# Expert gates of a product-key mixture: one 256-column matmul a token for both parts of the gate

## The chip, the cores and the metric

One core of a Trainium2 chip runs the whole program in one launch. The metric is device time in microseconds (us), a median over runs. A profiled execution of the same program gives the rows shown below.

## What is computed

The reference is a stack of layers on 256 tokens of width 1024 (retention, differential attention, feed-forward blocks, a recurrent mixer), all in float32. Two of its layers hold a product-key expert block, and only that block is touched here:

```python
q = (xc @ w_q).reshape(PEER_CHUNK, PEER_HEADS, 2, half)
sc = jnp.einsum('thpd,hpnd->thpn', q, subkeys)
s1, i1 = lax.top_k(sc[:, :, 0], PEER_TOPK)
s2, i2 = lax.top_k(sc[:, :, 1], PEER_TOPK)
cand = s1[..., :, None] + s2[..., None, :]          # best 16 of 256 per head
...
gate = jax.nn.softmax(top, axis=-1)
act = jax.nn.gelu(jnp.einsum('ted,td->te', u_e, xc))
return jnp.einsum('te,ted->td', gate * act, v_e)
```

There are 8 heads with 16 experts each, so every token has 128 slots; the experts form a 128 x 128 grid (i1, i2).

## The kernel before

The kernel computes the activations of all 16,384 experts densely and multiplies them by a gate that is zero for experts not chosen. `H` is an SBUF tile of 128 partitions (i1) x 128 rows (i2) x 256 tokens in float32. The method `peer` runs once for each of the two layers, in these stages:

- **Query stage.** 16 weight units through `gemm_a`, key scores and the first top-k (`route_keys`).
- **Expert stage, called the u stage here.** A loop over `i2` from 0 to 127. Each unit is one 128 x 1024 weight block, loaded by a DMA into one of four `raw` buffers and split by `split` into a high part `wh` (ScalarE, L122) and a low part `wl` (VectorE, L123) in three buffers each. `gemm_a` (L144 to L146) then does 24 matmuls of 256 columns into a `mm` accumulator (two banks). A gelu on ScalarE (L1234, L1236) empties it into `H`, or, for tokens whose gate is there already, into the buffer `ge`, which VectorE multiplies onto `H` (L1237).
- **Routing**, spread over units 2 to 43 (`route`): it ends with `rt["T"]`, four float16 values for each slot and token: i1, i2, and the gate's high and low part.
- **Gates**, from unit 44 on: 64 groups of four tokens per layer. `onehots` builds, for four tokens at once, the one-hot of i1 (`o1`), the one-hot of i2 (`o2`) and its products with the two gate parts (`oh`, `ol`), all 128 slots x 128 x 4 tokens in float16 with the token innermost. `gates` then does, for each token, two matmuls of 128 columns that add up in one accumulator: `o1` is the stationary operand, `oh` and `ol` are the moving ones. Because the token is innermost, both operands are read at a step of four float16 values, 8 bytes. The four tokens share one `aux` bank. One unit later `apply(k)` reads that bank twice: VectorE multiplies it onto the `k` rows of `H` that exist (L1441), ScalarE copies the remaining rows (L1444), to be multiplied when their unit's gelu comes.
- **Value stage.** 128 units of `peer_v`, with `H` as stationary operand (L1260) and four `acc` banks.

Each engine runs its instructions in the order of its own queue. That order comes from a planner that simulates the program; the splits have priority over what surrounds them (`AHEAD`). All weight DMAs go through SyncE's queue (SP), in order. Routing uses the part of `H` from row `K0` = 44 on as scratch memory (`carve`), since those rows are not filled yet; `consts_peer` loads three constant tables at the start of the block.

Of the kernel before, what the change touches and what calls it, by code (L numbers as in the profile page):

```python
# [67 lines left out]
class Ker:  # L68
# [27 lines left out]
    def psum(s, ctx, mm, aux, acc):  # L96

        for n, c in (("mm", mm), ("aux", aux), ("acc", acc)):
            setattr(s, "p" + n, ctx.enter_context(
                s.tc.tile_pool(name=f"ps_{n}", bufs=c, space=PSUM, reuse_waits="tile")))  # L100
        s.naux = aux
        s.cyc = ([s.aux, s.mm, s.aux] if aux > 2 else [s.aux, s.mm])
        s.psn = 0
# [1058 lines left out]
    def peer(s, l, xs, units_q, units_u, units_v, ln):  # L1162
        nc, A = s.nc, s.A
        with ExitStack() as cx:
            s.psum(cx, 2, 2, 4)
            hp = s.pool("peer_h", 1, cx)
            H = hp.tile([128, NKEYS, T], F32, name="H")
            cu = ExitStack()
            po = s.pool("peer_oh", 2, cu)
            p = s.pool("peer_u", 1, cu)  # L1170
            p2 = s.pool("peer_u2", 2, cu)
            s.consts_peer(p)
            xT = s.x_transposed(p, xs, "xT", s.ln_cols(ln), p2)

            off = [K0 * T]

            def carve(shape, dt=F32):
# [7 lines left out]
                if len(shape) == 2:  # L1185
# [2 lines left out]
                return ap.rearrange("p (%s) -> p %s" % (" ".join(names), " ".join(names)),  # L1188
                                    **{k: v for k, v in zip(names, shape[1:])})

            def restart():
                off[0] = K0 * T

            carve.restart = restart
            qT = carve([128, 16, T])
# [14 lines left out]
            for c in range(16):  # L1210
                ps = bank(c)
                s.gemm_a(next(units_q), xT, ps)
                nc.scalar.activation(qT[:, c], ps, AF.Copy)
                if c == 2:
                    scores(0)
                if c > 1:
                    scores(c - 1)
                    s.route_keys(rt, sc, c - 2)
            route = s.route(carve, p, rt)
            g = 0  # L1220
            pend = []
            for i2 in range(NKEYS):
# [7 lines left out]
                if nt == 0:  # L1230
                    nc.scalar.activation(H[:, i2], ps, AF.Gelu_apprx_tanh)
                else:
                    if nt < T:
                        nc.scalar.activation(H[:, i2, nt:], ps[:, nt:], AF.Gelu_apprx_tanh)  # L1234
                    ge = p2.tile([128, T], F32, name="ge")
                    nc.scalar.activation(ge[:, :nt], ps[:, :nt], AF.Gelu_apprx_tanh)  # L1236
                    nc.vector.tensor_tensor(H[:, i2, :nt], H[:, i2, :nt], ge[:, :nt], op=ALU.mult)  # L1237
                if 2 <= i2 < K0:
# [5 lines left out]
                elif i2 >= K0:  # L1244
                    for f in pend:
                        f(i2 + 1)
                        g += 1
                    e = (i2 + 2 - K0) * (T // 4) // (NKEYS - KEND - K0)
                    pend = [s.gates(H, s.onehots(p, po, rt, j * 4), j) for j in range(g, min(e, T // 4))]
            assert g * 4 == T  # L1250
            cu.close()
            p2 = s.pool("peer_v2", 3, cx)
            p = s.pool("peer_v", 1, cx)
            accs = [[s.acc(), s.acc()], [s.acc(), s.acc()]]
# [154 lines left out]

    def onehots(s, p, p2, rt, t0):  # L1410

        nc = s.nc
        sh = [128, 128, 4]

        def tok(j):
            return rt["T"][:, j, t0:t0 + 4][:, None, :].to_broadcast(sh)

        o1 = p2.tile(sh, F16, name="o1")
        o2 = p.tile(sh, F16, name="o2")
        oh = p2.tile(sh, F16, name="oh")  # L1420
        ol = p2.tile(sh, F16, name="ol")
        nc.vector.tensor_tensor(o1, s.iota4, tok(0), op=ALU.is_equal)
        nc.vector.tensor_tensor(o2, s.iota4, tok(1), op=ALU.is_equal)
        nc.vector.tensor_tensor(oh, o2, tok(2), op=ALU.mult)
        nc.vector.tensor_tensor(ol, o2, tok(3), op=ALU.mult)
        return o1, oh, ol

    def gates(s, H, oh3, g):


        nc = s.nc
        o1, oh, ol = oh3
# [12 lines left out]

        return apply

    def consts_peer(s, p):
        nc, A = s.nc, s.A
        s.iota4 = p.tile([128, 128, 4], F16, name="iota4")  # L1450
        nc.sync.dma_start(s.iota4, A["iota4"])
        s.cst_route = p.tile([128, 3, TOPK, TOPK], F16, name="croute")
        nc.sync.dma_start(s.cst_route, A["croute"])
        s.ident16 = p.tile([128, 128], F16, name="ident16")
        nc.sync.dma_start(s.ident16, A["ident16"])


def units_a(w):
# [187 lines left out]
```

## Time and profile before

| | us |
|---|---|
| median of 3 runs (2763.41 to 2766.23) | 2764.84 |
| the profiled execution | 2760.64 |
| its span, first to last instruction | 2758.5 |

Busy times of an engine are sums over its instructions. Matmuls are pipelined: a matmul's duration is its way through the array, and the next one starts before it ends, so the rate is read from the distance of the starts. PE is the matmul side of TensorE, PEld its weight loads, DVE VectorE, ACT ScalarE, SPq the DMA issues of SyncE.

### The profile page before, as it was taken

The page shows a single profiled execution, that of the slowest core. Times are in us where ns is not written, and L with a number is a line of the kernel's source. Part 1 is how long each engine was busy: PE and PEld are TensorE (multiplying, and loading weights), DVE is VectorE, ACT ScalarE, POOL GpSimd, SP SyncE. Part 2 cuts the span into 40 slices and gives each one's busy share as a digit, 9 for nine tenths or more (in the row PEclk, how much of TensorE's full clock was granted, in tenths as well). Part 3 has the DMA queues.
Part 4 walks back from the last instruction along what each step waited for, and adds up shares of the span by engine and source line. Part 5 has one row for each costly group of instructions (what it writes and reads, how often), then busy time and mean ns, then how long its engine had stood idle before and what let it go on. Part 6 is the DMA issues. An engine that isn't in the chain of part 4 may idle for free. (4 is left out here: it accounts for less than half of the span.)

```text
span 2758.5 us, 44974 instructions
## 1 busy us (share of the span) xinstructions
PE 2721.0 (99%) x17062; PEld 2420.3 (88%) x17062; DVE 1944.3 (70%) x3816; ACT 1391.1 (50%) x2443; POOL 7.7 (0%) x24
## 2 busy tenths in 40 slices
PE   9999999999999999999999999999999999999999
PEld 7789999999888888789999998888878887888887
DVE  7559967778666668789767787666677667665774
ACT  4445544444555555555444445555555555443554
POOL 0000000000000000000000000000000000000000
PEclk9999999999999999999999999999999999999999
DMA  6454554444666555345544445566655653221554
GB/s 214 158 183 162 180 181 146 146 146 146 199 194 195 193 194 168 101 160 179 178 154 148 142 150 190 192 193 196 191 176 188 190 176 110 75 70 62 175 187 150
DMA packets 124423, 450.74 MB, mean 163 GB/s; under 512 B 14080, under 2 KB 15120, under 8 KB 123952
## 3 DMA queue, kind: packets, MB, share of 16 engines
q1 hardware_dynamic: 124064, 447.81, 50.4%
q8 instruction: 134, 2.20, 0.3%
q14 instruction: 81, 0.66, 0.1%
q10 hardware_dynamic: 144, 0.07, 0.0%
HBM read 446.76 MB, written 1.05 MB: 162 GB/s over the span
## 5 line engine op out<-in xcount | busy, mean ns | idle before, releaser
L123 DVE TENSOR_TENSOR wl<-raw,wh 128x1024 fp32r<-128x1024 f32 x830 | 1015.7, 1224 | 464.5 <-ACT wh L122 463.2
L122 ACT ACTIVATE wh<-raw 128x1024 fp32r<-128x1024 f32 x830 | 879.7, 1061 | 836.9 <-PE mm L145 495.7
L144 PE MATMUL mm<-xT,wh 128*128 128x256 f32 x2384 | 682.9, 287 | 3.2 <-ACT ge L256 2.3
L146 PE MATMUL mm<-xT,wl 128*128 128x256 f32 x2384 | 678.6, 285 | 1.8 <-DVE wl L123 1.8
L145 PE MATMUL mm<-xT,wh 128*128 128x256 f32 x2384 | 678.3, 285 | 0.0
L144 PEld LDWEIGHTS mm<-xT,wh 128*128 128x128 f32 x2384 | 456.7, 192 | 5.5 <-ACT ge L256 2.7
L146 PEld LDWEIGHTS mm<-xT,wl 128*128 128x128 f32 x2384 | 456.3, 191 | 2.7 <-DVE wl L123 2.4
L145 PEld LDWEIGHTS mm<-xT,wh 128*128 128x128 f32 x2384 | 456.6, 192 | 0.7 <-DVE xT L258 0.3
L1260 PE MATMUL acc<-wl,gh 128*128 128x512 f32 x1024 | 317.3, 389 | 0.3
L1260 PE MATMUL acc<-wh,gl 128*128 128x512 f32 x1024 | 317.0, 389 | 0.0
L1260 PE MATMUL acc<-wh,gh 128*128 128x512 f32 x1024 | 277.0, 389 | 0.0
L1269 ACT ACTIVATE gh<-H 128x256 fp32r<-128x256 f32 x256 | 106.9, 418 | 297.4 <-PE acc L1260 297.4
L1260 PEld LDWEIGHTS acc<-wl,gh 128*128 128x128 f32 x1024 | 192.3, 188 | 40.9 <-DVE wl L123 1.1
L1260 PEld LDWEIGHTS acc<-wh,gl 128*128 128x128 f32 x1024 | 192.2, 188 | 39.8
L1260 PEld LDWEIGHTS acc<-wh,gh 128*128 128x128 f32 x1024 | 192.1, 188 | 39.7
L1270 DVE TENSOR_TENSOR gl<-H,gh 128x256 fp32r<-128x256 f32 x256 | 108.8, 425 | 115.5 <-PE acc L1260 115.0
L156 PE MATMUL mm<-xT,wh 128*128 128x512 f32 x406 | 145.9, 397 | 0.8 <-ACT wh L122 0.6
L1436 PE MATMUL aux<-ol,o 128*128 128x128 f16 x512 | 128.6, 297 | 0.0
L1435 PE MATMUL aux<-oh,o 128*128 128x128 f16 x512 | 127.2, 294 | 0.0
L157 PE MATMUL mm<-xT,wl 128*128 128x256 f32 x406 | 114.2, 281 | 0.8 <-DVE wl L123 0.8
L156 PE MATMUL aux<-xT,wh 128*128 128x512 f32 x294 | 105.0, 394 | 0.0
L179 PE MATMUL acc<-wl,xT 128*128 128x512 f32 x256 | 103.2, 404 | 0.0
(540 smaller groups left out, 3921.6 us busy)
## 6 DMA issues: line engine op xcount, KB each, us to landing
raw<-peer_u SPq DMA_DIRECT2D x256, 512.0 KB, 3.7
raw<-peer_v SPq DMA_DIRECT2D x256, 512.0 KB, 4.5
raw<-ffn_w SPq DMA_DIRECT2D x132, 512.0 KB, 4.5
raw<-peer_q SPq DMA_DIRECT2D x32, 512.0 KB, 4.2
raw<-ret_qk SPq DMA_DIRECT2D x16, 512.0 KB, 5.1
raw<-ret_v SPq DMA_DIRECT2D x16, 512.0 KB, 3.6
raw<-ret_g SPq DMA_DIRECT2D x16, 512.0 KB, 4.4
raw<-ret_o SPq DMA_DIRECT2D x16, 512.0 KB, 4.2
```

What stands on the lines that cost most here:

```text
L122: a = nc.scalar.activation(h, ap, AF.Copy)
L123: d = nc.vector.tensor_tensor(l, ap, h.bitcast(F32), op=ALU.subtract)
L144: nc.tensor.matmul(out, w[0][:, c], x[0][:, d], start=start and d == 0, stop=False)
L145: nc.tensor.matmul(out, w[0][:, c], x[1][:, d], start=False, stop=False)
L146: nc.tensor.matmul(out, w[1][:, c], x[0][:, d], start=False, stop=stop and d == ND - 1)
L156: nc.tensor.matmul(ps, w[0][:, c], x, start=d == 0, stop=False)
L157: nc.tensor.matmul(ps[:, :T], w[1][:, c], both[:, d, 0], start=False, stop=False)
L1260: mm = nc.tensor.matmul(accs[cb][tt], a[:, t], b[:, cb * 512:cb * 512 + 512], start=i2 == 0 and wi == 0, stop=i2 == NKEYS - 1 and wi == 2)
L1269: a = nc.scalar.activation(wh, H[:, i2], AF.Copy).ins
L1270: d = nc.vector.tensor_tensor(wl, H[:, i2], wh.bitcast(F32), op=ALU.subtract).ins
L1435: nc.tensor.matmul(ps[:, t], o1[:, :, t], oh[:, :, t], start=True, stop=False)
L1436: nc.tensor.matmul(ps[:, t], o1[:, :, t], ol[:, :, t], start=False, stop=True)
```

## The change

Both gate parts of a token go through one matmul of 256 columns, into separate halves of a 256-column result, in place of two matmuls of 128 columns that add up. The parts are summed afterwards: ScalarE scales one into a new SBUF buffer `gt` (128 x 512, one copy), VectorE adds the other to it, multiplies `H` by the sum, and ScalarE copies the remaining rows from `gt` in place of the accumulator. A group of four tokens now takes two PSUM banks; two such pairs come from the four `acc` banks, given back after the query stage and taken again for the value stage. The one-hots are made by two VectorE instructions of 1024 elements in place of four of 512. To make room, `croute` and `ident16` move into the scratch part of `H` (so their DMAs are issued beside that of the subkeys), the two temporaries of the transposes are given back before the one-hots are allocated, and the gelu buffer becomes single.

```diff
-            s.psum(cx, 2, 2, 4)
+            cq = ExitStack()
+            s.psum(cx, 2, 2, 4, cq)
...
-            po = s.pool("peer_oh", 2, cu)
             p = s.pool("peer_u", 1, cu)
-            p2 = s.pool("peer_u2", 2, cu)
-            s.consts_peer(p)
-            xT = s.x_transposed(p, xs, "xT", s.ln_cols(ln), p2)
+            s.iota4 = p.tile([128, 128, 4], F16, name="iota4")
+            nc.sync.dma_start(s.iota4, A["iota4"])
+            with ExitStack() as ct:
+                xT = s.x_transposed(p, xs, "xT", s.ln_cols(ln), s.pool("peer_t", 2, ct))
+            po = s.pool("peer_oh", 2, cu)
...
+            s.cst_route = carve([128, 3, TOPK, TOPK], F16)
+            nc.sync.dma_start(s.cst_route, A["croute"])
+            s.ident16 = carve([128, 128], F16)
+            nc.sync.dma_start(s.ident16, A["ident16"])
...
+            cq.close()
+            cg = ExitStack()
+            s.banks(cg, "gat", 2)
             route = s.route(carve, p, rt)
...
-                    ge = p2.tile([128, T], F32, name="ge")
+                    ge = p.tile([128, T], F32, name="gelu")
...
             cu.close()
+            cg.close()
+            s.banks(cx, "acc", 4)
...
-        sh = [128, 128, 4]
+        sh = [128, 2, 128, 4]
         def tok(j):
-            return rt["T"][:, j, t0:t0 + 4][:, None, :].to_broadcast(sh)
-        o1 = p2.tile(sh, F16, name="o1")
...
-        nc.vector.tensor_tensor(o1, s.iota4, tok(0), op=ALU.is_equal)
-        nc.vector.tensor_tensor(o2, s.iota4, tok(1), op=ALU.is_equal)
-        nc.vector.tensor_tensor(oh, o2, tok(2), op=ALU.mult)
-        nc.vector.tensor_tensor(ol, o2, tok(3), op=ALU.mult)
+            return rt["T"][:, j:j + 2, t0:t0 + 4][:, :, None, :].to_broadcast(sh)
+        o = p2.tile(sh, F16, name="o12")
+        og = p2.tile(sh, F16, name="og")
+        nc.vector.tensor_tensor(o, s.iota4[:, None].to_broadcast(sh), tok(0), op=ALU.is_equal)
+        nc.vector.tensor_tensor(og, o[:, 1:2].to_broadcast(sh), tok(2), op=ALU.mult)
+        return o[:, 0], og
...
-        ps = s.aux().rearrange("p (t i) -> p t i", t=4)
+        ps = s.pgat.tile([128, 4, 2, 128], F32, name="gat")
         for t in range(4):
-            nc.tensor.matmul(ps[:, t], o1[:, :, t], oh[:, :, t], start=True, stop=False)
-            nc.tensor.matmul(ps[:, t], o1[:, :, t], ol[:, :, t], start=False, stop=True)
-        pv = ps.rearrange("p t i -> p i t")
+            nc.tensor.matmul(ps[:, t], o1[:, :, t], og[:, :, :, t], start=True, stop=True)
+        pv = ps.rearrange("p t a i -> p a i t")
+        gt = p.tile([128, NKEYS, 4], F32, name="gate")
+        nc.scalar.activation(gt, pv[:, 1], AF.Copy, scale=1.0 / GSCALE)
         def apply(k):
-            nc.vector.scalar_tensor_tensor(H[:, :k, ts], pv[:, :k], 1.0 / GSCALE, H[:, :k, ts],
-                                           op0=ALU.mult, op1=ALU.mult)
+            nc.vector.scalar_tensor_tensor(gt, pv[:, 0], 1.0 / GSCALE, gt, op0=ALU.mult, op1=ALU.add)
+            nc.vector.tensor_tensor(H[:, :k, ts], H[:, :k, ts], gt[:, :k], op=ALU.mult)
             if k < NKEYS:
-                nc.scalar.activation(H[:, k:, ts], pv[:, k:], AF.Copy, scale=1.0 / GSCALE)
+                nc.scalar.activation(H[:, k:, ts], gt[:, k:], AF.Copy)
```

## Rows read from the trace of the kernel before

**Rows 1.** Busy time in the first gate stretch: length, PE, PEld, DVE, ACT, POOL.
```profile
405.00:688.00 283.00, 283.00 (x2368) 279.72 (x2368) 217.16 (x457) 121.96 (x296) 0.00 (x0) 1.00 0.45 146
```

**Rows 2.** Timeline of PE and PEld over one group of gates (start, length).
```profile
470.70 0.28 PE L145 MATMUL mm<-xT,wh 128*128 128x256 f32 x1
...
476.22 0.28 PE L146 MATMUL mm<-xT,wl 128*128 128x256 f32 x1
476.34 0.28 PE L1435 MATMUL aux<-oh,o 128*128 128x128 f16 x1
476.45 0.30 PE L1436 MATMUL aux<-ol,o 128*128 128x128 f16 x1
...
477.16 0.29 PE L1436 MATMUL aux<-ol,o 128*128 128x128 f16 x1
477.41 0.29 PE L145 MATMUL mm<-xT,wh 128*128 128x256 f32 x1
...
476.34 0.11 PEld L1435 LDWEIGHTS <-o 128*128 128x128 f16 x1
476.35 0.13 PEld L1436 LDWEIGHTS <-o 128*128 128x128 f16 x1
```

**Rows 3.** Timeline of PE: 16-bit matmuls with contiguous operands.
```profile
211.06 1.47 PE L267 MATMUL mm<-zeros 128*128 128x256 bf16 x12
1353.01 0.34 PE L1406 MATMUL aux<-ident,H 128*128 128x128 f16 x3
```

**Rows 4.** Timeline of PE in the value stage: 512-column matmuls, first and last of eleven distances.
```profile
799.75 0.39 PE L1260 MATMUL acc<-wh,gl 128*128 128x512 f32 x1
...
802.25 0.62 PE L1260 MATMUL acc<-wh,gl 128*128 128x512 f32 x2
```

**Rows 5.** Groups of PE by form: gate matmuls and float16 transposes (xcount, busy, mean ns).
```profile
L1435 PE MATMUL aux<-oh,o 128*128 128x128 f16 x512 | 127.2, 294 | 0.0
L1406 PE MATMUL aux<-ident,H 128*128 128x128 f16 x16 | 2.3, 224 | 0.0
```

**Rows 6.** Groups of DVE in the first gate stretch; then durations of three kinds.
```profile
L123 DVE TENSOR_TENSOR wl<-raw,wh 128x1024 fp32r<-128x1024 f32 x80 | 97.8, 1222 | 28.1 <-ACT wh L122 27.9
L1422 DVE TENSOR_TENSOR o<-iota,slotT 128x512 f16<-128x512 f16 x60 | 25.3, 421 | 21.1 <-PE aux L1436 21.1
L1424 DVE TENSOR_TENSOR oh<-o,slotT 128x512 f16<-128x512 f16 x60 | 25.3, 421 | 18.0 <-PE aux L1435 18.0
...
L1441 DVE SCALAR_TENSOR_TENSOR H<-aux,H x128: 343/511/679, 407.9 to 1676.6; 128x184 f32<-128x184 f32 x2, 128x188 f32<-128x188 f32 x2, 128x192 f32<-128x192 f32 x2, 128x200 f32<-128x200 f32 x2
L1237 DVE TENSOR_TENSOR H<-H,ge 128x112 f32<-128x112 f32 x4 | 1.1, 266 | 0.0
L1237 DVE TENSOR_TENSOR H<-H,ge 128x212 f32<-128x212 f32 x4 | 1.5, 374 | 0.0
L1382 DVE TENSOR_TENSOR H<-H,croute x4: 1219/1224/1244, 309.4 to 1315.3; 128x2048 f16<-128x2048 f16 x4
```

**Rows 7.** Timeline of DVE late in the stage and at the group of rows 2.
```profile
660.66 0.42 DVE L1422 TENSOR_TENSOR o<-iota,slotT 128x512 f16<-128x512 f16 x1
661.00 0.42 DVE L1425 TENSOR_TENSOR ol<-o,slotT 128x512 f16<-128x512 f16 x1
...
471.68 1.22 DVE L123 TENSOR_TENSOR wl<-raw,wh 128x1024 fp32r<-128x1024 f32 x1
```

**Rows 8.** Groups of ACT in the first gate stretch; one form of L1444.
```profile
L122 ACT ACTIVATE wh<-raw 128x1024 fp32r<-128x1024 f32 x79 | 83.9, 1062 | 162.0 <-PE mm L145 158.7 <-issue 3.3
...
L1444 ACT ACTIVATE H<-aux 128x320 f32<-128x320 f32 x2 | 0.9, 443 | 0.0
```

**Rows 9.** SP's queue and ACT at the start of the first expert block.
```profile
213.29 0.33 SPq L1198 DMA_DIRECT2D H<-subkeys  x1
214.16 25.72 SPq L133 DMA_DIRECT2D raw<-peer_q  x9
...
224.94 1.05 ACT L122 ACTIVATE wh<-raw 128x1024 fp32r<-128x1024 f32 x1
```

More of the change, by code (lines that the diff above doesn't have):

```diff
@@ L94, in pool, with banks, psum @@
         return (ctx or s.ctx).enter_context(s.tc.tile_pool(name=name, bufs=bufs, reuse_waits="tile"))
-    def psum(s, ctx, mm, aux, acc):
+    def banks(s, ctx, n, c):
+        setattr(s, "p" + n, ctx.enter_context(
+            s.tc.tile_pool(name=f"ps_{n}", bufs=c, space=PSUM, reuse_waits="tile")))
+    def psum(s, ctx, mm, aux, acc, ctx_acc=None):
         for n, c in (("mm", mm), ("aux", aux), ("acc", acc)):
-            setattr(s, "p" + n, ctx.enter_context(
-                s.tc.tile_pool(name=f"ps_{n}", bufs=c, space=PSUM, reuse_waits="tile")))
+            s.banks(ctx_acc or ctx if n == "acc" else ctx, n, c)
         s.naux = aux
@@ L1168, in peer @@
             cu = ExitStack()
+            p = s.pool("peer_u", 1, cu)
+            s.iota4 = p.tile([128, 128, 4], F16, name="iota4")
+            nc.sync.dma_start(s.iota4, A["iota4"])
+            with ExitStack() as ct:
+                xT = s.x_transposed(p, xs, "xT", s.ln_cols(ln), s.pool("peer_t", 2, ct))
             po = s.pool("peer_oh", 2, cu)
-            p = s.pool("peer_u", 1, cu)
-            p2 = s.pool("peer_u2", 2, cu)
-            s.consts_peer(p)
-            xT = s.x_transposed(p, xs, "xT", s.ln_cols(ln), p2)
             off = [K0 * T]
@@ L1189, in carve @@
                                     **{k: v for k, v in zip(names, shape[1:])})
+            s.cst_route = carve([128, 3, TOPK, TOPK], F16)
+            nc.sync.dma_start(s.cst_route, A["croute"])
+            s.ident16 = carve([128, 128], F16)
+            nc.sync.dma_start(s.ident16, A["ident16"])
+            free = off[0]
             def restart():
-                off[0] = K0 * T
+                off[0] = free
             carve.restart = restart
@@ L1248, in peer @@
                     e = (i2 + 2 - K0) * (T // 4) // (NKEYS - KEND - K0)
-                    pend = [s.gates(H, s.onehots(p, po, rt, j * 4), j) for j in range(g, min(e, T // 4))]
+                    pend = [s.gates(H, p, s.onehots(p, po, rt, j * 4), j) for j in range(g, min(e, T // 4))]
             assert g * 4 == T
             cu.close()
+            cg.close()
+            s.banks(cx, "acc", 4)
             p2 = s.pool("peer_v2", 3, cx)
@@ L1412, in onehots @@
         nc = s.nc
-        sh = [128, 128, 4]
+        sh = [128, 2, 128, 4]
         def tok(j):
-            return rt["T"][:, j, t0:t0 + 4][:, None, :].to_broadcast(sh)
-        o1 = p2.tile(sh, F16, name="o1")
-        o2 = p.tile(sh, F16, name="o2")
-        oh = p2.tile(sh, F16, name="oh")
-        ol = p2.tile(sh, F16, name="ol")
-        nc.vector.tensor_tensor(o1, s.iota4, tok(0), op=ALU.is_equal)
-        nc.vector.tensor_tensor(o2, s.iota4, tok(1), op=ALU.is_equal)
-        nc.vector.tensor_tensor(oh, o2, tok(2), op=ALU.mult)
@@ L1425, in onehots, with gates @@
-        nc.vector.tensor_tensor(ol, o2, tok(3), op=ALU.mult)
-        return o1, oh, ol
-    def gates(s, H, oh3, g):
+            return rt["T"][:, j:j + 2, t0:t0 + 4][:, :, None, :].to_broadcast(sh)
[4 more added lines that the diff above has]
+        return o[:, 0], og
+    def gates(s, H, p, oh2, g):
@@ L1431, in gates @@
         nc = s.nc
-        o1, oh, ol = oh3
-        ps = s.aux().rearrange("p (t i) -> p t i", t=4)
+        o1, og = oh2
+        ps = s.pgat.tile([128, 4, 2, 128], F32, name="gat")
         for t in range(4):
-            nc.tensor.matmul(ps[:, t], o1[:, :, t], oh[:, :, t], start=True, stop=False)
-            nc.tensor.matmul(ps[:, t], o1[:, :, t], ol[:, :, t], start=False, stop=True)
-        pv = ps.rearrange("p t i -> p i t")
+            nc.tensor.matmul(ps[:, t], o1[:, :, t], og[:, :, :, t], start=True, stop=True)
@@ L1443, in apply @@
             if k < NKEYS:
-                nc.scalar.activation(H[:, k:, ts], pv[:, k:], AF.Copy, scale=1.0 / GSCALE)
+                nc.scalar.activation(H[:, k:, ts], gt[:, k:], AF.Copy)
         return apply
[L1448 to L1455, printed above, removed]
```

## Prediction

> **What bounds the kernel now.** The first view is the busy time of each engine in the stretch that the change touches. PE is busy for all 283.0 us of it, DVE for 217.2 and ACT for 122.0 [rows 1]; the second layer's gates have a stretch like it. So TensorE sets the pace there, at the full 2.4 GHz (granted clock 1.00), and the question is not what an instruction costs but how far apart PE's instructions start. The second view is therefore the timeline of PE over one group of gates. The expert matmuls start 0.120 us apart (46 distances in 5.52 us), and the eight gate matmuls, with half as many columns, 0.118 us (0.71 us for six distances) [rows 2]. A group takes 476.34 to 477.29, since the second expert matmul after it starts at 477.41 and each takes 0.12: 0.95 us, which is 8 x 0.1183. For 128 groups in two layers that is 121 us, and this is all that the change can draw on. The views of DVE and ACT come next, because the change gives both more work; what the reader is to see there is whether that stays under the time that PE leaves.
>
> **Why a gate matmul takes 0.118 us.** Everything hangs on this. Either the weight load sets the distance, and then half of the loads save half of the time; or the 128 moving columns do, and then 256 of them take about as long as two matmuls took. Four rows speak for the columns. First, the first two loads of a group end at 476.45 and 476.48 (0.11 after 476.34, 0.13 after 476.35) [rows 2]: two loads 0.03 us apart are not what holds matmuls 0.118 apart. Second, with contiguous operands three float16 matmuls of 128 columns, each with its own load, take 0.34 us from the start of the first to the end of the last; less one duration of 0.224 that leaves a distance of 0.058 [rows 3, 5]. The gate matmuls differ from these in the 8-byte step. Third, a gate matmul also lasts longer, 0.294 against 0.224 [rows 5], and these 0.070 are close to the 0.060 by which the distance is longer: the data itself comes in more slowly. Fourth, the last gate matmul has the contiguous load of an expert matmul behind it and still holds the array until 477.29, 0.13 after its start [rows 2].
>
> So the price of one new matmul, 256 columns at the same step, is not in the trace, and I bound it. From above: twice the old distance, 0.237. From below, if the loads were the limit after all: 0.118. Between them stands the nearest row. 128 columns at a step of 8 bytes span 1024 bytes of a partition, as 256 float32 columns do, and both take 0.118 to 0.120. 256 such columns span 2048 bytes, as 512 float32 columns do, and those start 0.2273 us apart (2.50 us for eleven) [rows 4]. I take 0.227. The fixed part of about 0.011 us of each matmul is then all that is saved.
>
> The Trainium skill speaks for the other side. In SBUF — State Buffer, Door 1, its note on cachelines says that two accesses to the same 16-byte line are enough for full bandwidth, and a step of 8 bytes gives two; in TensorE: Matmul & The Clock Gate, LDWEIGHTS, a load is put at its columns over 1.2 GHz, an estimate of 107 ns here. By both, the loads would be the limit and the change would save half of 121 us. The rows above disagree with both: 0.03 us between two loads, and a longer stream.
>
> **PE, the sum.** Before, a group takes 8 x 0.1183 = 0.947 us; after, 4 x 0.2273 = 0.909 us. The gain is 0.038 us for each of 128 groups, 4.9 us. With 0.1183 and the step from 256 to 512 float32 columns, 0.107, it would be 4 x 0.2256 and 5.7 us; with 0.237 nothing. Accumulators in two banks cost PE nothing that I can see: each result lies within one bank, and two pairs are in turn as two `aux` banks were.
>
> **VectorE.** Back to back, an instruction starts 0.08 us before the duration of the one ahead is over (0.34 apart for 0.42) [rows 7], so I count durations less 0.08. Old, a group: four one-hot instructions at 0.34 and the product from PSUM at 0.511 - 0.08 [rows 6], 1.79 us. New: one-hots of 1024 elements lie between 512 at 0.421 and 2048 at 1.224 [rows 6]; 0.522 ns an element gives 0.69, twice 0.61. The sum of the parts has 512 elements, the longest of L1441, 0.679, so 0.60. The product on `H` has 4k elements, 336 in the mean: with 0.374 at 212 and 0.266 at 112 that is 0.51, so 0.43 (0.62 for k = 128) [rows 6]. Together 2.25 us, 0.46 more, 29 us in a layer. DVE goes from 217 to 246 us of some 281. Late in the stage it is tighter: a unit there has a split (1.222 - 0.08), a gelu product of up to 0.34 and 64 groups for 82 units, 0.78 x (1.22 + 0.60 + 0.62) = 1.90: 3.38 us, where PE has 24 x 0.120 + 0.78 x 0.909 = 3.59. So DVE stays below PE, by 6% at the end and by over 20% at the beginning. What covers it: weights are split early. The `wl` that ends at 472.90 goes into the third of three buffers and is wanted by the unit at 477.21 [rows 2, 7], 4.3 us later, so DVE may be late by three instructions and more.
>
> **ScalarE.** The new copy of 512 elements into `gt`: from 0.443 at 320 and 1.062 at 1024 [rows 8] I work out 0.61; the old copy stays, from another source. 64 x 0.53 is 34 us more on 122, 156 of 281. Two waits are new. The copy waits for the gate matmuls, and, `gt` being single, for the product of the group before. Behind it in ACT's queue stand gelus, which free the `mm` banks, and the next `wh`. But ACT waits 158.7 us in this stretch for PE to give weight buffers back [rows 8], so a microsecond of waiting is taken from that. The single gelu buffer works the same way: a gelu waits for the product of the one before, and PE has the second `mm` bank meanwhile. I price both at nothing; if the cover goes, they cost what the waiting rival below costs.
>
> **Moved steps.** The tables `croute` and `ident16` go into `H`, so their two DMAs stand beside that of the subkeys (213.29) in SP's queue, ahead of the fifth weight load of the block (214.16). At up to 0.87 us from one issue to the next, two of them put that load off by 1.7 us at most; its `wh` begins at 224.94 [rows 9], so ten microseconds cover it. The PSUM banks change hands between stages: gates after the query stage, and the value stage after the last group, which is applied two units before the end. Neither has a waiter nearby. Zero.
>
> **The sum.** The profiled execution takes 2760.64 us with a span of 2758.5; less 4.9 that is 2755.7 and 2753.6. The median is 4.2 us above the profiled execution, and less 4.9 it is 2759.9. About 0.2% (5.5 us) is what a measurement of this kernel can tell from no change, so this forecast lies on the near side of that line.
>
> **The rivals.**
> - *The loads are the limit, chance 0.08.* Then a matmul stays at 0.118 and PE saves 512 x 0.118 = 60 us. DVE would give a little back: 3.38 us a unit late in the stage against 2.88 + 0.78 x 0.473 = 3.25, at most 0.13 for some 20 units twice, 5 us. Time: about 2710. For it: a load lasts 0.11 to 0.13, as long as the distance [rows 2]. Against it: the four rows above.
> - *Loads and stream share the reads, chance 0.07.* If each distance held 0.033 of load and 0.085 of stream, the new matmul would take 0.203 and 512 x (0.237 - 0.203) = 17 us would go, to 2747. Against it: the last gate matmul, with no gate load behind it, is no shorter.
> - *Waits on DVE decide, slower, chance 0.20.* Today DVE waits 21.1 + 18.0 us in 60 groups for PE to give one-hot buffers back [rows 6], 0.65 us a group, 0.51 a unit. If these waits stayed as they are, because the order in the queue puts the one-hots as early as now, DVE would need 3.89 us a unit at the end against 3.59 of PE. It decides from 0.27 us of such waits a group on, at the end; at the full 0.65 it holds in the second half, at 0.15 us in the mean for 41 units in two layers, 12 us. With PE's gain 2772; with half of the waits about 2763. Against it: a DVE that is later finds the buffers free.
> - *The new one-hots lose their rate, chance 0.04.* At L1441's 1.02 ns an element (0.343 at 184, 0.679 at 512) a one-hot instruction takes 1.20, 1.12 spaced, and a late unit 4.2 us; in the mean 3.65 against 3.59, some 0.6 over in the second half: 50 us, 2810. Against it: L1382, also with broadcast operands in three dimensions, keeps 0.6 ns an element.
> - *The change brings nothing, because 256 columns take 0.237*: part of the main case; 2765.
>
> **How the numbers follow.** The main case, loads hidden and DVE covered, has 0.55 and its own range is 2758 to 2766; the remaining 0.06 is for an order of the queues that I don't foresee, on either side. Faster by over 0.2% (below 2759.3): the two upper rivals, 0.15, a third of the main case, 0.18, and 0.02 of the remainder, 0.35. Slower by over 0.2% (above 2770.4): over half of the waiting rival, 0.12, the rate, 0.04, and 0.03 of the remainder, 0.19. Within: 0.46. The range 2745 to 2776 leaves out the loads rival, the rate rival and the end of the waiting one, about 0.16.
>
> **What would show it.** Right: the gate matmuls are 512 of 256 columns, 0.227 us apart, each lasting longer than now by about 0.11; PE without idle time in both stretches; DVE busy for some 246 of 279 us, its waits for one-hot buffers shorter; the sum of the parts at 0.68 us and the copy into `gt` at 0.61. Wrong: a distance of 0.118 to 0.20, then the loads were in it; idle time on PE ahead of L144 or L146 that ends with `wl` or a gelu, then DVE or ACT is late; one-hot instructions of 1.1 us; a later fifth load that PE waits for in the query stage.

## The result, and the profile after

The changed kernel takes 2783.18 us in the median (2780.57 to 2786.32, 4 runs) against 2764.91 (2763.41 to 2766.23) of the kernel before in the same session: a ratio of 1.0067, interval 1.0049 to 1.0084, so 18.3 us slower. Forecast were 2759.9 us, with a range of 2745 to 2776. The profiled execution took 2780.57 us with a span of 2778.8, 20.3 more than the span before.

Busy time in the first gate stretch (length, PE, PEld, DVE, ACT, POOL, granted clock, DMA share, GB/s), then PE at one group of gates, four matmuls merged into one line:

```profile
405.00:688.00 283.00, 280.28 (x2118) 257.31 (x2117) 241.53 (x391) 156.01 (x352) 0.00 (x0) 1.00 0.45 147
```
```profile
473.12 0.28 PE L149 MATMUL mm<-xT,wl 128*128 128x256 f32 x1
473.25 1.09 PE L1448 MATMUL gat<-og,o 128*128 128x256 f16 x4
473.98 0.48 PE L147 MATMUL mm<-xT,wh 128*128 128x256 f32 x1
```

PE was busy throughout before [rows 1]; now it lacks 2.7 us here. The matmuls themselves did what was forecast: four of 0.407 us mean duration end 1.09 us after the start of the first, so they stand (1.09 - 0.407) / 3 = 0.228 us apart (over all groups the median distance is 0.230), where two of 128 columns took 0.237 [rows 2]. Groups of the same stretch, with the idle time ahead of them and its releaser:

```profile
L1455 DVE SCALAR_TENSOR_TENSOR gate<-gat,gate 128x512 f32<-128x512 f32 x60 | 41.1, 684 | 0.0
L1437 DVE TENSOR_TENSOR o<-iota,slotT 128x1024 f16<-128x1024 f16 x58 | 40.1, 692 | 31.2 <-PE gat L1448 31.0
L1438 DVE TENSOR_TENSOR og<-o,slotT 128x1024 f16<-128x1024 f16 x58 | 39.7, 684 | 0.0
L1452 ACT ACTIVATE gate<-gat 128x512 f32<-128x512 f32 x60 | 35.8, 596 | 15.1 <-DVE H L1456 11.5 <-DVE H L1251 3.1
```

Each price is close to its forecast: one-hots 0.69 and 0.68 (0.69), the sum 0.684 (0.68), the copy 0.596 (0.61). New is the end of the last line: the copy into `gt` waits for VectorE. The waits of the stage up to the value matmuls (engine, line, releaser: us in all, times, longest):

```profile
ACT wh L125 <- PE mm L148: 107.2, 80, 2.3
ACT gate L1452 <- DVE H L1456: 13.3, 17, 2.0
ACT gelu L1250 <- DVE H L1251: 4.6, 5, 1.7
ACT H L1458 <- DVE gate L1455: 4.2, 3, 2.2
PEld mm L147 <- ACT gelu L1250: 3.6, 4, 1.4
PE mm L147 <- ACT gelu L1250: 1.8, 3, 0.9
PE gat L1448 <- DVE gate L1455: 1.4, 2, 0.8
```

ScalarE waits for VectorE, and TensorE for ScalarE; twice TensorE waits for VectorE itself, for the sum that frees a pair of banks (1.4 us, the last line). One place of the first kind, in the timelines of DVE, ACT and PE:

```profile
648.98 0.61 DVE L1456 TENSOR_TENSOR H<-H,gate 128x444 f32<-128x444 f32 x1
...
651.00 0.68 DVE L1455 SCALAR_TENSOR_TENSOR gate<-gat,gate 128x512 f32<-128x512 f32 x1
...
653.87 0.37 DVE L1251 TENSOR_TENSOR H<-H,gelu 128x212 f32<-128x212 f32 x1
```
```profile
649.71 0.60 ACT L1452 ACTIVATE gate<-gat 128x512 f32<-128x512 f32 x1 [1.99 <-DVE H L1456]
650.20 0.34 ACT L1250 ACTIVATE gelu<-mm 128x212 f32<-128x212 f32 x1
...
651.87 0.19 ACT L1248 ACTIVATE H<-mm 128x44 f32<-128x44 f32 x1
...
653.79 1.06 ACT L125 ACTIVATE wh<-raw 128x1024 fp32r<-128x1024 f32 x1 [1.58 <-PE mm L148]
...
654.83 0.59 ACT L1452 ACTIVATE gate<-gat 128x512 f32<-128x512 f32 x1
655.31 0.35 ACT L1250 ACTIVATE gelu<-mm 128x212 f32<-128x212 f32 x1
```
```profile
653.71 1.09 PE L1448 MATMUL gat<-og,o 128*128 128x256 f16 x4
655.71 0.39 PE L147 MATMUL mm<-xT,wh 128*128 128x256 f32 x1 [0.92 <-ACT gelu L1250]
```

DVE works from 647.84 to 654.24 without a gap. The copy of 649.71 waits 1.99 us for the product of the group before it (648.98 and 0.61 long), and the gelu of 650.20 stands behind it. VectorE multiplies that gelu onto `H` only at 653.87, 3.3 us after its read was done, and until then the single gelu buffer is taken. The next unit's first part is read from its `mm` bank at 651.87, its second part only at 655.31, behind a split (653.79) and a copy (654.83); so TensorE, done with the gate matmuls, finds the bank taken and idles for 0.92 us. (The 1.99 us did not last by themselves: ScalarE waits for TensorE again before 653.79.) There are six waits in this stage, 4.76 us idle and 6.1 us with the refilling after each. The last of them stands before the first value matmul:

```profile
703.06 0.28 PE L149 MATMUL mm<-xT,wl 128*128 128x256 f32 x1
704.95 0.50 PE L1276 MATMUL acc<-wh,gh 128*128 128x512 f32 x1 [1.61 <-ACT gh L1285]
```

**Where the 20.3 us lie.** For one measure over all runs I count in the trace's matmuls: from the start of the 2450th expert matmul ahead of a value stage to the first value matmul. This *gate stage* holds all 64 groups of a layer and little else. It takes 354.7 us before and 359.4 after, in both layers: 9.4 us. (The first one begins 345.5 us into the span in both kernels.) The *tail*, from the last value matmul of the second layer to the end, holds nothing that the change touches, and yet went from 729.1 to 737.9: 8.8 us. Another 1.7 lie between the layers (from the last value matmul of the first to the first of the second, 632.4 and 638.8, less the 4.7 of the gate stage in it), and 0.4 in the value stages. The clock took part: of the tail, 17.1 us ran at half the clock (1.2 GHz) against 3.4 before (the last 2 to 3 us, at half clock in every run, are left out here and below). Ahead of one of these falls, from 2310 to 2326, TensorE was busy for 12.85 of 16 us. Between the layers 6.8 us ran at half clock against none before; e4 below has the changed kernel's instructions and no half clock there, and all but 0.2 of the 1.7 us are gone. A late stretch, before and then after, with the granted clock behind the counts:

```profile
2330.00:2390.00 60.00, 59.22 (x363) 48.54 (x363) 40.09 (x82) 35.09 (x82) 1.50 (x4) 1.00 0.28 88
```
```profile
2330.00:2390.00 60.00, 59.46 (x315) 45.54 (x314) 33.41 (x77) 29.36 (x73) 1.50 (x4) 0.91 0.22 71
```

### The profile page after: what moved, and what is told of

Same layout as the page of the kernel before. It is cut to its first block, busy times and chain, and to the rows that moved or that the text cites. A ratio compares the mean times of both kernels' runs of the same rounds, so it can differ in the third digit from the quotient of the medians.

```text
span 2778.8 us, 43988 instructions
## 1 busy us (share of the span) xinstructions
PE 2730.4 (98%) x16550; PEld 2382.0 (86%) x16550; DVE 2003.5 (72%) x3688; ACT 1467.7 (53%) x2571; POOL 7.8 (0%) x24
## 5 line engine op out<-in xcount | busy, mean ns | idle before, releaser
L1448 PE MATMUL gat<-og,o 128*128 128x256 f16 x512 | 137.7, 407 | 2.7 <-DVE gate L1455 2.7
L1437 DVE TENSOR_TENSOR o<-iota,slotT 128x1024 f16<-128x1024 f16 x128 | 88.3, 691 | 65.2 <-PE gat L1448 64.8
```

What stands on the lines that cost most here:

```text
L1448: nc.tensor.matmul(ps[:, t], o1[:, :, t], og[:, :, :, t], start=True, stop=True)
```

## The experiments

| kernel | median us | gate stage us | tail us | of it at half clock us |
|---|---|---|---|---|
| before | 2764.9 | 354.7 | 729.1 | 3.4 |
| changed | 2783.2 | 359.4 | 737.9 | 17.1 |
| e1 moving columns contiguous | 2708.8 | 328.0 | 732.0 | 10.2 |
| e2 stationary columns contiguous | 2763.6 | 353.2 | 734.1 | 17.1 |
| e3 products by VectorE, contiguous | 2763.8 | 352.4 | 734.0 | 13.7 |
| e4 copy written later | 2784.7 | 359.4 | 740.1 | 23.9 |
| e5 two buffers for gelu | 2784.2 | 362.6 | 734.0 | 13.7 |
| e6 before, 45 idle matmuls | 2771.3 | 354.7 | 729.8 | 6.8 |
| e7 before, 24 idle matmuls | 2775.5 | 354.7 | 737.7 | 17.1 |
| e8 changed, two narrow matmuls | 2778.5 | 356.5 | 741.2 | 27.3 |
| e9 another sum, two buffers for the copy | 2785.5 | 362.2 | 741.5 | 27.3 |
| e10 products by ScalarE, contiguous | 2741.9 | 339.2 | 737.5 | 17.1 |
| e11 no gate copy | 2778.3 | 359.8 | 737.7 | 23.9 |
| e12 products split | 2718.0 | 329.8 | 737.1 | 23.9 |
| e13 no sum | 2765.9 | 355.1 | 729.5 | 3.4 |

Gate stage, tail and clock are those of the profiled execution. e1, e2, e6 and e7 ran once.

**What sets the distance of the gate matmuls: e1, e2.** In the kernel before, one operand at a time is read as contiguous columns of the same tile; the other numbers that it then reads make other gates.

```diff
-nc.tensor.matmul(ps[:, t], o1[:, :, t], oh[:, :, t], start=True, stop=False)
+c = slice(t * 128, t * 128 + 128)
+nc.tensor.matmul(ps[:, t], o1[:, :, t], fh[:, c], start=True, stop=False)   # e1; fl likewise
+nc.tensor.matmul(ps[:, t], f1[:, c], oh[:, :, t], start=True, stop=False)   # e2; ol likewise
```


> The kernel before, with one thing changed: the 128 moving columns of a gate matmul are read from contiguous addresses (the wrong elements of the same tiles, so the gates of this kernel are not those of the reference), while the stationary operand keeps its 8-byte step. Stream theory (the step of the moving operand sets the distance of 0.118 us): the distance falls to 0.056 to 0.070 us, a group from 0.95 to about 0.5 us, and 128 groups make the run some 55 us shorter, about 2710 us. Load theory (the strided weight load sets it): the distance stays 0.118 and the time 2765 us.

> The kernel before, with the stationary operand of a gate matmul read from contiguous addresses (wrong elements, so its gates are not those of the reference) and the moving operand at its 8-byte step. Stream theory: the distance stays 0.118 us and the time 2765 us; the load itself lasts 0.10 instead of 0.117 us. Load theory: the distance falls to about 0.06 us and the time to about 2710 us.

e1: 2708.75 us, 55 less; e2: 2763.55, the same as before (2763.91 in that session). PE at a group of e1:

```profile
471.79 0.22 PE L1437 MATMUL aux<-oh,o 128*128 128x128 f16 x1
471.84 0.22 PE L1438 MATMUL aux<-ol,o 128*128 128x128 f16 x1
471.90 0.22 PE L1437 MATMUL aux<-oh,o 128*128 128x128 f16 x1
471.95 0.22 PE L1438 MATMUL aux<-ol,o 128*128 128x128 f16 x1
```

The distance fell from 0.118 to 0.056 with each load still there and still strided. So the step of the moving columns sets the distance, as the prediction argued from four rows, and merging two matmuls into one could not give much. e2 shows what the loads' step is worth: 1.5 us a stage.

**Products written contiguous by VectorE: e3.** In the kernel before, the four instructions per group become one for `o1` and eight that compare and multiply in one go, each writing one token's 128 contiguous columns.

```diff
-nc.vector.tensor_tensor(oh, o2, tok(2), op=ALU.mult)
-nc.vector.tensor_tensor(ol, o2, tok(3), op=ALU.mult)
...
+for t in range(4):
+    for o, j in ((oh, 0), (ol, 1)):
+        nc.vector.tensor_scalar(o[:, t], s.iota, rt["T"][:, 1, t0 + t:t0 + t + 1],
+                                rt["T"][:, 2 + j, t0 + t:t0 + t + 1], op0=ALU.is_equal, op1=ALU.mult)
```


> A version that computes the right gates with contiguous moving columns: the gate parts of each token are made by one VectorE tensor_scalar of 128 elements per token and part (eight a group, compare with i2 and multiply by the gate part) into tiles with the token outermost; the one-hot of i1 stays as it was, and so do the two matmuls of 128 columns, the accumulator and what reads it. Stream theory: matmul distance 0.056 to 0.070 us, about 55 us less, 2710 us, if the eight small instructions stay under the 1.02 us of the three that they replace (0.13 us each); at 0.2 us each VectorE would need 3.5 us a late unit against 3.3 of TensorE and give part of it back, 2725 us. Load theory: 2765 us or more.

2763.77 us (2762.17 to 2765.58), ratio 1.0001 (0.9991 to 1.0010). The groups and the waits show where e1's gain went:

```profile
L1420 DVE TENSOR_SCALAR ol<-iota,slotT 128x128 f16<-128x128 f16 x240 | 69.8, 312 | 0.0
```
```profile
PEld mm L144 <- ACT ge L1236: 11.0, 10, 1.6
PE mm L144 <- ACT ge L1236: 9.3, 10, 1.4
```
```profile
405.00:695.00 290.00, 278.69 (x2452) 269.90 (x2452) 267.58 (x766) 125.63 (x306) 0.00 (x0) 1.00 0.46 149
```

128 elements cost 312 ns on VectorE, 480 times in this stretch, where the expectation had 0.13 us, and 0.2 as the case in which part of the gain is given back. DVE is at 267.58 of 290 us, and TensorE waits for gelu reads, as in the changed kernel, though nothing here touches ScalarE's gate work. That was the first sign that VectorE was the cause. Of the 24.4 us by which this gate stage is longer than e1's, 12.7 are idle time of TensorE; besides, 214 of the 1024 gate matmuls stand alone between expert matmuls, and what that costs was not measured by itself.

**The waits on ScalarE and the single buffers: e4, e5, e9.** All three are the changed kernel. e4 writes the copy in `apply`, ahead of the sum. e5 gives the gelu two buffers; `gt` stays single, and to make room VectorE builds the two one-hots by an instruction each, three a group in place of two. e9 copies the low part as float16 into one of two buffers and sums in the bank; its gelu buffer stays single.

```diff
# e4
-gt = p.tile([128, NKEYS, 4], F32, name="gate")
-nc.scalar.activation(gt, pv[:, 1], AF.Copy, scale=1.0 / GSCALE)
 def apply(k):
+    gt = p.tile([128, NKEYS, 4], F32, name="gate")
+    nc.scalar.activation(gt, pv[:, 1], AF.Copy, scale=1.0 / GSCALE)
# e5
+p2 = s.pool("peer_u2", 2, cu)
...
-ge = p.tile([128, T], F32, name="gelu")
+ge = p2.tile([128, T], F32, name="gelu")
...
-nc.vector.tensor_tensor(o, s.iota4[:, None].to_broadcast(sh), tok(0), op=ALU.is_equal)
+nc.vector.tensor_tensor(o1, s.iota4, tok(0)[:, 0], op=ALU.is_equal)
+nc.vector.tensor_tensor(o2, s.iota4, tok(0)[:, 1], op=ALU.is_equal)
# e9, where p is a pool of two buffers
-gt = p.tile([128, NKEYS, 4], F32, name="gate")
-nc.scalar.activation(gt, pv[:, 1], AF.Copy, scale=1.0 / GSCALE)
+lo = p.tile([128, NKEYS, 4], F16, name="glo")
+nc.scalar.activation(lo, pv[:, 1], AF.Copy)
...
+nc.vector.tensor_tensor(pv[:, 0], pv[:, 0], lo, op=ALU.add)
```


> The changed kernel with one thing moved: ScalarE's copy of one part into the single buffer gate is issued in apply, one unit later, just ahead of the sum that needs it, instead of right behind the gate matmuls. Theory of the single buffer: ScalarE's waits on the product of the group before (13 us a layer) go, the gelus queued behind no longer hold the mm banks, and the stalls of TensorE in the gate stretch fall from 6.1 us a layer to under 2.5; the first expert block ends 3.5 to 5 us earlier than in the changed kernel. Rival (VectorE is simply too full): the stalls stay at 5 us a layer or grow.

> The changed kernel with two gelu buffers as before the change (room for it comes from a single one-hot of i2, made by its own instruction: three VectorE instructions a group, of 512, 512 and 1024 elements, in place of two of 1024). Theory of the single gate buffer: little changes, since what holds the gelus is the copy into gate ahead of them; the stalls stay between 4 and 7 us a layer. Rival (the single gelu buffer is the cause): the stalls fall under 2.5 us a layer.

> The changed kernel with ScalarE's copy of one part in float16 in two buffers of half the size, and the sum made in place in PSUM by VectorE; the wide matmul stays. Theory of the single gate buffer: ScalarE's waits for the product of the group before (13 us a layer) go and with them the gelus' lateness: stalls of TensorE in the gate stretch under 2.5 us a layer instead of 6.1, the first value stage begins 3.5 us or more earlier than in the changed kernel. Rival (VectorE, 256 us busy of 301, is late whatever buffers there are): stalls of 5 us and more a layer.

e4 tells nothing apart: the planner put out the same order of instructions, and 2784.67 us (ratio 1.0082, 1.0065 to 1.0099) is a second measurement of the changed kernel. e5 takes 2784.17 us (1.0081, 1.0065 to 1.0098), e9 2785.48 (1.0082, 1.0065 to 1.0099); their gate stages are longer by 3 us, not shorter. Waits of e5, then of e9:

```profile
ACT gate L1455 <- DVE H L1459: 18.1, 18, 2.4
PEld mm L147 <- ACT gelu L1251: 9.7, 9, 1.4
```
```profile
ACT glo L1453 <- PE gat L1449: 37.5, 28, 2.3
ACT gelu L1251 <- DVE H L1252: 10.6, 6, 1.8
PEld mm L147 <- ACT gelu L1251: 8.7, 6, 1.5
```

With a second gelu buffer the wait stands at the copy into the single `gt`, with a second buffer for the copy it stands at the gelu: it moves to the next instruction that needs VectorE. So neither single buffer is the cause by itself. No run doubles both, and e5 gives VectorE one more instruction a group, so these runs do not rule out that the two make the waits together; e11, e8 and e13 below bear on it.

**The parts of the change: e8, e11, e13.** e8 is the changed kernel with two matmuls of 128 columns into one bank again and the readers of before; the merged one-hots, the moved tables and the single gelu buffer stay. e11 takes only ScalarE's copy away, e13 the copy and the sum; in both the low part of the gate is left out, and in e11 a constant table stands in its place.

```diff
# e8
-    nc.tensor.matmul(ps[:, t], o1[:, :, t], og[:, :, :, t], start=True, stop=True)
+    nc.tensor.matmul(ps[:, t], o1[:, :, t], og[:, 0, :, t], start=True, stop=False)
+    nc.tensor.matmul(ps[:, t], o1[:, :, t], og[:, 1, :, t], start=False, stop=True)
...
# e11
-nc.scalar.activation(gt, pv[:, 1], AF.Copy, scale=1.0 / GSCALE)
...
-    nc.vector.scalar_tensor_tensor(gt, pv[:, 0], 1.0 / GSCALE, gt, op0=ALU.mult, op1=ALU.add)
+    nc.vector.scalar_tensor_tensor(gt, pv[:, 0], 1.0 / GSCALE, s.iota4, op0=ALU.mult, op1=ALU.add)
# e13 (e8 likewise, from its one bank)
-    nc.vector.tensor_tensor(H[:, :k, ts], H[:, :k, ts], gt[:, :k], op=ALU.mult)
+    nc.vector.scalar_tensor_tensor(H[:, :k, ts], pv[:, 0, :k], 1.0 / GSCALE, H[:, :k, ts],
+                                   op0=ALU.mult, op1=ALU.mult)
```


> The changed kernel with two 128-column matmuls a token into one accumulator bank, and its two readers, as before; the merged one-hots, the moved tables and the single gelu buffer stay. Theory (the split of the result over ScalarE and VectorE makes the stalls): TensorE's stalls in the gate stretch go, the first value stage begins within 0.7 us of the kernel before, and the time is 2764 us with a clock as before, up to 2772 with more half-clock stretches. Rival (merged one-hots or the single gelu buffer make them): 3 us or more of stalls a layer stay.

> The changed kernel without ScalarE's copy of the low part of the gate: VectorE's sum takes a constant table (0 to 127) as its second term in its place, so the low part is left out and the gates are other numbers; the matmuls, VectorE's sum (685 ns) and product stay. It tells ScalarE's part of the stalls from VectorE's. Theory A (ScalarE's in-order queue: the gate copy waits for VectorE with a gelu read behind it, and TensorE then waits for the bank that the gelu read frees): the matmuls that wait for gelu (L147) and those that wait for the sum (L1448) in the changed kernel, 3.15 us idle per layer, go, and only the 1.6 us before the first value matmul stays: the first value matmul starts at about 700.5 to 702 (704.9 in the changed kernel), about 2776 us in all. Theory B (VectorE's own length, sum and product one after the other, frees the banks late): the stalls stay at 4 us or more per layer, and the first value matmul starts at 704 to 706, about 2783 us in all.

> The changed kernel without the summing of the two parts: neither ScalarE's copy nor VectorE's sum, the product on H reads the high part from its bank, and the low part of the gate is left out. The 256-column matmuls and the two-bank accumulators stay. Theory B (VectorE's length: the sum's 44 us per stage make it late): TensorE waits for nothing in the gate stage but the 1.6 us before the first value matmul, so against e8, whose matmuls are two of 128, the first value matmul comes some 1.4 us earlier (64 times 0.022 us), at 700.4 to 701.5, and VectorE is busy some 221 of 298 us. Theory C (the wide matmul or the accumulators over two banks hold TensorE up, whatever VectorE does): waits of 3 us or more in matmuls ahead of the value stage, and the first value matmul at 703.5 to 705. In both the stages behind the gates cost some 8 to 12 us more than in the kernel before, as in e8, so that the whole comes out at about 2775 or 2781 us.

e8: 2778.53 us (ratio 1.0057, 1.0040 to 1.0074), above the 2764 to 2772 of its theory, since its tail is 12.1 us longer than that of the kernel before. e11: 2778.28 (1.0054, 1.0039 to 1.0070). e13: 2765.86 (1.0008, 0.9997 to 1.0018). The expectation of e13 had 2775 or 2781, with a tail like e8's, and it has none such. The gate stages part them. Busy time in 405 to 703, of the changed kernel, e8 and e13, then waits of e11 and of e13:

```profile
405.00:703.00 298.00, 294.85 (x2226) 270.39 (x2225) 254.14 (x409) 164.08 (x371) 0.00 (x0) 1.00 0.45 147
```
```profile
405.00:703.00 298.00, 296.39 (x2476) 292.71 (x2475) 221.03 (x350) 132.18 (x313) 0.00 (x0) 1.00 0.45 148
```
```profile
405.00:703.00 298.00, 296.40 (x2229) 272.62 (x2228) 220.68 (x353) 132.00 (x315) 0.00 (x0) 1.00 0.46 149
```
```profile
ACT gelu L1250 <- DVE H L1251: 7.0, 4, 2.1
PEld mm L147 <- ACT gelu L1250: 6.6, 7, 1.0
PE mm L147 <- ACT gelu L1250: 2.9, 7, 0.4
```
```profile
PEld acc L1276 <- ACT gh L1285: 1.8, 1, 1.8
PE acc L1276 <- ACT gh L1285: 1.6, 1, 1.6
```

e11 refutes my theory of the time, the copy in ScalarE's queue: without the copy TensorE still idles 2.9 us within the stage (3.2 in the changed kernel) and the stage takes 359.8, since the gelu now waits for VectorE's gelu product directly. In e8 and e13, with 33 us less on DVE, nothing is left but the wait before the first value matmul; both keep the single gelu buffer, and e13 has the wide matmuls and the two banks. So these cost nothing by themselves; VectorE's sum does. (No run took away the sum and left the copy, which would have had no reader, and none parts the sum's length from its place in VectorE's queue.) The wait before the first value matmul, 1.6 us idle, costs 1.8: 356.5 of e8 less 354.7. e13 then shows PE's gain by itself: 355.1 less 1.8 is 353.3, and 354.7 less that is 1.4 us a stage; against e8 it is 1.4 too.

**The tail: e6, e7.** The kernel before, with idle matmuls (of 0.11 us) written behind the first layer's value stage. The planner spread them over the first part of that stage (704.3 to 788.8 us in e6, 704.9 to 729.4 in e7), which gets 5.8 and 3.0 us longer, so that all that follows starts later.

```diff
+            s.keep_clock(24 if l == 0 else 0)   # e7; 45 in e6
```


> The kernel before, with 45 matmuls on a tile of zeros (0.109 us each, 4.9 us) at the end of the first expert block, ahead of the normalisation: all that follows runs 4.9 us later, as in the changed kernel. Theory that the clock is an effect of timing: stretches at half clock appear in the later stages that the change doesn't touch, as in the changed kernel, and the run takes more than 4.9 us longer, up to 2780 us. Rival (what is lost behind the first expert block comes from the changed code or from another order of the queues): the granted clock stays at 0.999 and the time is 2770 us.

> The same with 24 matmuls, 2.6 us. Theory of timing: granted clock and time need not lie between those of none and 45; any loss beyond 2.6 us goes with stretches at half clock at sparse places of the later stages. Rival: 2767.5 us and a clock of 0.999.

2771.32 us with 45 matmuls and 2775.49 with 24: 8.1 and 12.3 above the kernel before, where the matmuls themselves add 4.9 and 2.6. The smaller delay costs more: e6's tail is 0.7 us longer than before, e7's 8.6. In the order of instructions e6's tail is almost that of before, e7's almost that of the changed kernel (99.7% of PE's sequence alike, told by the shapes of its instructions; before and changed, 97.4%). The table then shows two lines. With before's order the tail is 729.1, 729.8, 732.0, 734.1 and 737.1 us for 3.4, 6.8, 10.2, 17.1 and 23.9 us at half clock (before, e6, e1, e2, e12); with the changed kernel's order it is 737.5 to 737.9 at 17.1, 740.1 at 23.9 and 741.2 and 741.5 at 27.3 (e10, e7, changed; e4; e8, e9). At 17.1 the changed order goes with 3.4 to 3.8 us more, and 13.7 us more at half clock go with 5.0 (e2 against before). A third order (e13, and nearly so e3, e5 and e11) lies close to the first: 729.5 at 3.4, 734.0 at 13.7, 737.7 at 23.9. Each point is one execution. The planner picks these orders anew for each kernel.

**ScalarE makes contiguous products: e10, e12.** The changed kernel with the accumulators and their readers as before the change (the moved tables and the single gelu buffer stay), and with products written token by token: in e10 all eight of a group by ScalarE, in e12 those of three tokens by ScalarE and the fourth's two in one instruction of VectorE. The lines are shown against the kernel before.

```diff
-nc.vector.tensor_tensor(oh, o2, tok(2), op=ALU.mult)
-nc.vector.tensor_tensor(ol, o2, tok(3), op=ALU.mult)
+for t in range(3):          # e12; 4 in e10, without the VectorE line
+    for a in range(2):
+        nc.scalar.activation(og[:, t, a], o2[:, :, t], AF.Copy, scale=rt["S"][:, a, t0 + t:t0 + t + 1])
+nc.vector.tensor_tensor(og[:, 3], o2[:, :, 3][:, None, :].to_broadcast([128, 2, 128]),
+                        rt["S"][:, :, t0 + 3][:, :, None].to_broadcast([128, 2, 128]), op=ALU.mult)
...
-    nc.tensor.matmul(ps[:, t], o1[:, :, t], oh[:, :, t], start=True, stop=False)
+    for a in range(2):
+        nc.tensor.matmul(ps[:, t], o1[:, :, t], og[:, t, a], start=a == 0, stop=a == 1)
```


> A version of its own: contiguous moving columns, made by ScalarE. VectorE makes the two one-hots; ScalarE multiplies the one-hot of i2 by each gate part, token by token (eight copies of 128 elements a group with a scale per partition), into a tile with the token outermost; two 128-column matmuls a token add up in one bank as before the change. Stream theory: matmul distance 0.056 to 0.07 us, a group 0.47 to 0.5 us; ScalarE gets 64 x 8 x 0.16 = 82 us a layer and stays under 210 of 255; VectorE loses 2 x 0.34 a group. About 50 us less, 2710 to 2720 us. Rival (ScalarE's queue, which also frees the mm banks, becomes the bound): 2740 us or more.

> As e10 (contiguous products, two matmuls of 128 columns, the accumulators as before the change), but of the four tokens of a group ScalarE makes three tokens' products and VectorE the fourth's in one instruction of 256 elements. If e10 lost its remainder against e1 (13.7 us per gate stage) to a full ScalarE (274.6 of 298 us busy), taking a quarter of its 437 ns products away (some 41 us of issue time a stage) for some 25 us more on VectorE (203 of 298 us busy) gives back 5 to 12 us per stage: the first value matmul at 674 to 681 (685.8 in e10), 2718 to 2732 us in all. If the loss is the chain from one-hot to product to matmul, whoever makes it, the time stays within 5 us of e10's 2741.9.

e10: 2741.92 us (ratio 0.9929, 0.9913 to 0.9946). e12: 2717.97 us (2714.30 to 2724.59; 0.9834, 0.9821 to 0.9848), faster than both kernels by 45 and 65 us. Busy time of e10, then of e12:

```profile
405.00:680.00 275.00, 268.87 (x2449) 265.32 (x2448) 189.17 (x342) 262.57 (x787) 0.00 (x0) 1.00 0.48 157
```
```profile
405.00:660.00 255.00, 255.00 (x2343) 252.42 (x2342) 198.05 (x390) 223.63 (x647) 0.00 (x0) 1.00 0.50 162
```

In e10 ACT is busy for 262.57 of 275 us and sets the pace: a product lasts 0.437 us in the mean, where the expectation counted 0.16. With a quarter of the products moved, PE is busy throughout, and the gate stage is 329.8 us: e1's 328.0 and the 1.8 before the first value matmul.

## Why the prediction was wrong

**The matmuls: right.** Forecast were 0.227 us, measured 0.230 in the median, and the reason (the stream, not the loads) is shown by e1 and e2. Both rivals that let the loads count are refuted; a load lasts as long as the old distance [rows 2], but that is no sign that it sets it, since e1 halves the distance with the same loads. The gain came out smaller: a group from the end of the matmul ahead to the end of the one behind fell from 1.073 to 1.051, 0.022 us and not 0.038, which is 2.8 us in all instead of 4.9. The price was off by some 0.003 for each of four matmuls, 0.011 of the 0.016 us that are missing, and the rest is the passage into and out of the group.

**The step that failed: the cover for a late VectorE**, "so DVE may be late by three instructions and more", and with it "I price both at nothing", the waits that the change puts into ScalarE's queue. VectorE's sum costs 4.3 us in each stage (359.4 of the changed kernel less 355.1 of e13, which has neither copy nor sum; the 1.8 before the first value matmul stay open below), where 1.4 were gained. Of the two waits priced at nothing the copy's did not decide: without the copy (e11) the stage takes as long. The cover that I named (158.7 us in which ScalarE waits for weight buffers, 4.3 us between a split and its use) belongs to the weights. What came late were other readers: the gelu read that frees one of two `mm` banks, queued until VectorE had made the gelu product before it, and twice a stage the sum itself, which frees a pair of gate banks. These go through VectorE in its queue's order, and I checked VectorE only for its total over a unit. That total was right (241.5 us busy of 283; forecast were 246 of 281), and still the stage lost time.

**The rival on the slow side: the right engine, its wait not parted.** It had waits for one-hot buffers stay as long as they were, and 2772 us. They became shorter (31.0 us in 58 groups against 39.1 in 60 [rows 6]), but only by a fifth, and 0.53 us a group is above the 0.27 from which the rival let VectorE decide. In 505 to 700, where all idle times of TensorE within the stage lie, after and then before:

```profile
DVE o L1437 <- PE gat L1448: 19.8, 28, 1.4
```
```profile
DVE o L1422 <- PE aux L1436: 17.5, 19, 1.3
DVE oh L1424 <- PE aux L1435: 5.5, 6, 1.1
```

That is 19.8 us against 23.0, in the same queue as the sums and products. No run takes these waits away, so their share in the lateness is not shown. Without the sum (e13) they are longer, 53.8 us in 405 to 703 against 31.7 in the changed kernel, and TensorE waits for nothing within the stage. The rival's price (12 us less the gain of 4.9, where the gate stages lost 9.4) was near; that does not show its mechanism.

**Not foreseen: 8.9 of the 18.3 us** (18.3 less 9.4) lie outside the gate stages, for which the prediction had a chance of 0.06 and no size. In the profiled executions 8.8 lie in the tail, some 3.8 with another order of the same instructions and some 5 with the clock, by the comparisons above. e7 shows that 24 idle matmuls are enough to bring both about in a kernel whose gates are untouched. The clock is no accident of the two profiled executions: the four runs of the changed kernel have a granted clock of 0.993 to 0.995, those of the kernel before 0.995 to 0.999 in all sessions.

**Right at nothing:** the moved tables, since the gate stage begins when it did, and the two banks as such; e8 and e13 have both or one of them and no wait within the gate stage. Only with the late sum does TensorE wait for a pair.

**Open:** the 1.6 us before the first value matmul. It appears in e3, e5 and e8 to e13 as in the changed kernel, but not before or in e1, e2, e6 and e7; before and in e1 ScalarE's `gh` copies start before the value stage. The hand-over of the banks is not its cause, since e3, e10 and e12 have the banks of before. An order of the planner is the likely reason; it wasn't tried. Nor is it shown why the clock falls more often with some kernels.

## What to carry to other kernels

Before merging matmuls, measure what sets their distance: here it was the step between the moving columns, and reading them contiguous is worth 27 us a layer (e1), of which e12 keeps 25 with its products still to be made; the merge is worth 1.4. A wait is covered only if the instruction queued behind it is: follow each engine's queue from the new wait to the bank or buffer that the bottleneck needs next, and do not take a busy sum below the bottleneck's as proof. And where an order is planned anew for each version, look at stages that the change leaves alone before explaining a difference of some 10 us by the change.

## What the runs showed of the hardware

Float16 moving columns 8 bytes apart take 0.118 us for 128 and 0.230 for 256; contiguous ones 0.056 for 128, with the stationary operand strided all the while (e1). By the Trainium skill (SBUF — State Buffer, Door 1, the note on cachelines) two hits on a 16-byte line are enough for the full rate, and 8 bytes apart there are two; for TensorE's moving operand e1 disagrees, by a factor of two. (The same note lets each access that crosses to a new line pay, and in that direction the runs agree.) ScalarE's 128-element product from a source at 8-byte steps took 412 to 437 ns in the mean, VectorE's 256 elements with two broadcast operands 418, and VectorE's compare-and-multiply of 128 elements 312: per element the single instruction with more elements was the cheapest.
